# Low weight parts at another place within 64 bytes than the moving rows, in a hybrid encoder layer on one core

## The chip, the cores and the metric

The kernel runs on one core of a Trainium2 chip. The metric is the device time of one execution in microseconds, as the median of several runs.

## The reference

One layer: a gated Hyena branch (long convolution by FFT) and an attention branch on one normalised input, merged by sigmoid gates, projected, and followed by a SwiGLU FFN. All arrays are float32: 512 tokens, width 2048, FFN width 5632.

```python
h = rms_norm(x, mix_norm_g)
u_h, q, k, v, g = split(h @ w_in)
y_h = hyena(u_h)                        # short conv, product, long FFT conv, product
y_a = block_gqa_attention(rope(norm(q)), rope(norm(k)), v)
g_h, g_a = split(sigmoid(g + b_gate), 2)
x = x + (g_h * (y_h @ w_br_hyena) + g_a * (y_a @ w_br_attn)) @ w_out
h2 = rms_norm(x, ffn_norm_g)
return x + (silu(h2 @ w_ffn_gate) * (h2 @ w_ffn_up)) @ w_ffn_down
```

## The kernel before

All large products are made on TensorE in float32r, an operand being split into a high part and a low part (the rest). ScalarE copies the high part, VectorE subtracts it to get the low one, and TensorE multiplies high by high, high by low and low by high (`mm`, line 125). Weights come as tiles of 128x1024 numbers, eight blocks of 128x128, by DMAs on SyncE's queue (`raw` tiles).

Four stages use a scheme with seven products in place of eight, two by two blocks at a time (`seven`): the gates (names begin with g), the FFN's gate and up matrices (f), and the two halves of the FFN's down matrix (d and e). `run` goes through groups; a group takes four weight tiles (a11, a21, a22, a12), makes four sums of them on VectorE (`wsum`, line 868, tiles s), splits seven tiles (`wsplit`: ScalarE's copy on line 875, VectorE's subtraction on line 877), and runs seven products in three banks of PSUM called x, y and z. There are 15 groups in the gates, 44 in the FFN and 8 in each down half, so 75 groups and 525 products.

A product (`product`) has eight high matmuls, whose moving rows are 512 columns (256 of the high part of X and 256 of its low part, side by side), and eight low matmuls, whose weights are the low parts and whose moving rows are the 256 high columns. Each matmul has weights of its own, which are loaded ahead while the matmul before it streams. In the gates and in the FFN the order within a product turns from one product to the next (high, low; low, high; ...), but for the first and the last group; in the down halves it is always high, low. The instructions run in program order on each engine, and every split has a tile from a ring of three (`whi` and `wlo`, shared with the other stages, where `wblk` fills them).

Pools are filled from the left side of SBUF upwards and, later in the kernel, from the right side downwards. Each tile's place follows from what was allocated before it. Counting through the allocations, the tiles `wh`, `wl` and X all begin 32 bytes past a multiple of 64 bytes in every partition, and rows and blocks within them are multiples of 64 bytes long. (The word place means this remainder from here on.) One group of matmuls is otherwise: in the filters' transform (names kp), the constant tables CS, which are the weights there, lie at place 0, since a tile `fl` of 1296 bytes comes before them, and the moving rows kus and kvs lie at place 32. A small tile, `pad_t`, holds room on the right side.

Of the kernel before, what the change touches and what calls it, by code (L numbers as in the profile page):

```python
# [11 lines left out]
F32 = mybir.dt.float32  # L12
F32R = mybir.dt.float32r
# [4 lines left out]
P = 128  # L18
# [11 lines left out]
BLK = 8  # L30
# [16 lines left out]
O_ORDER = (4, 5, 6, 7, 8, 0, 9, 10, 11, 12, 1, 2, 3, 13, 14, 15)  # L47
STD_ORDER = (*range(EARLY_ACTS, NSTD), *range(EARLY_ACTS))
NEARLY = 5

C_X0, C_X1, C_HV, C_Q, C_KV, C_GH, C_GA = 0, 1024, 2048, 3072, 4096, 4608, 6656

# [54 lines left out]
def layer_kernel(tc, wpk, xT, par, flt, zemb, w4, decT, tbl, tb2, rope, qkg, out):  # L107
# [5 lines left out]
    wpool = tc.alloc_tile_pool(name="wpool", bufs=1)  # L113
# [46 lines left out]

    state = {"tile": 0, "pos": BLK, "hi": None, "lo": None}

    def wblk(nb=1):
        st = state
        if st["pos"] >= BLK:
            i = st["tile"]
            raw = wpool.tile([P, BLK * P], F32, tag="raw", bufs=2, name=f"wr{i}")
            hi = wpool.tile([P, BLK * P], F32R, tag="whi", bufs=3, name=f"wh{i}")
            lo = wpool.tile([P, BLK * P], F32R, tag="wlo", bufs=3, name=f"wl{i}")
            st.update(tile=i + 1, pos=0, hi=hi, lo=lo, raw=raw)  # L170

        i, n = st["tile"] - 1, {1: XW // 2, 2: XW}.get(st["tile"], BLK)
        if st["pos"] % n == 0:
            c = slice(st["pos"] * P, (st["pos"] + n) * P)
            nc.sync.dma_start(st["raw"][:, c], wpk[i, :, c])
            nc.scalar.copy(st["hi"][:, c], st["raw"][:, c])  # L176
            nc.vector.tensor_tensor(st["lo"][:, c], st["raw"][:, c], st["hi"][:, c].bitcast(F32), ALU.subtract)  # L177
        a = st["pos"] * P
        st["pos"] += nb
        return st["hi"][:, a:a + nb * P], st["lo"][:, a:a + nb * P]  # L180
# [6 lines left out]
    def group(ps, act, k0=0, k1=None):  # L187
        n = len(act)
        for k in range(k0, n if k1 is None else k1):
            wh, wl = wblk()  # L190
            mm3(ps, wh, wl, act[k][0], act[k][1], k == 0, k == n - 1)
            step()
# [312 lines left out]
    queue(mlp_gen())  # L505
    queue(filter_gen(0))
    w00 = wblk()
    for k in range(KT):
        xr = r3.tile([P, S], F32, tag="r", bufs=16, name=f"xr{k}")
        nc.sync.dma_start(xr, xT[k])  # L510
        hl = r1.tile([P, 2 * S], F32R, tag="hl", bufs=16, name=f"xh{k}")
        hi, lo = hl[:, :S], hl[:, S:]
        nc.scalar.activation(hi, xr, AF.Copy, scale=pcol("mixg", k))
        nc.vector.scalar_tensor_tensor(lo, xr, pcol("mixg", k), hi.bitcast(F32), ALU.mult, ALU.subtract)
        xg.append((hi, lo))
        for i in range(XW):
            wh, wl = wblk() if k + i else w00
            if k == 0:
                mm(xps[i], wh, hi, True, False)
                mm(xps[i], wl, hi, False, False)  # L520
                mm(xps[i], wh, lo, False, False)
            else:
                mm3(xps[i], wh, wl, hi, lo, False, k == KT - 1)
            step()
        sumsq_add(acc1, xr, k, "xsq", work)
# [88 lines left out]
    at = tc.alloc_tile_pool(name="at", bufs=1)  # L614
# [179 lines left out]
    def behind(ins):  # L794
        return tc.issue_after(ins) if ins else nullcontext()

    def seven(nm, gi, nv=3, turns=False):
# [25 lines left out]
        def x_tile(p):  # L823
            pool = xa if p < NEARLY else late["xb"][p - NEARLY]
            return pool.tile([P, 2 * SQ], F32R, tag="X", bufs=NEARLY if p < NEARLY else 1, name=f"{nm}X{p}")

# [13 lines left out]
        def x_split(p, V, cuts):  # L840
            xs[p] = x_tile(p)
            for a, b in zip(cuts, cuts[1:]):
                x_high(p, V, a, b)
                x_low(p, V, a, b)
# [20 lines left out]
        def wsum(name, a, b, ins=None):  # L865
            t = late["sg"].tile([P, BLK * P], F32, tag="sg", bufs=3, name=nm + name)
            with behind(ins):
                raws["sum"] = nc.vector.tensor_tensor(t, a, b, ALU.add).ins  # L868
            return t

        def wsplit(w, name, ins=None, low_ins=None):
            hi = wpool.tile([P, BLK * P], F32R, tag="whi", bufs=3, name=f"{nm}wh{name}")
            lo = wpool.tile([P, BLK * P], F32R, tag="wlo", bufs=3, name=f"{nm}wl{name}")
            with behind(ins):
                nc.scalar.copy(hi, w)  # L875
            with behind(low_ins):
                raws["wl"] = nc.vector.tensor_tensor(lo, w, hi.bitcast(F32), ALU.subtract).ins  # L877
            return hi, lo
# [31 lines left out]
        def run(groups, c_tiles, finish, rows=None, sums=None, side_pool=None, norm=None, tail=None, each=None, halves=False,  # L910
# [8 lines left out]
            def pool(name, **kw):  # L919
                return tc.alloc_tile_pool(name=nm + name, bufs=1, reuse_waits="tile", **kw)  # L920
# [7 lines left out]
            for n in range(groups):  # L928
# [4 lines left out]
                if tail and n == groups - 1:  # L933
                    next(tail)
                h11 = wsplit(w0["a11"], f"a11_{n}")
                if first:
                    for p in rows:
# [3 lines left out]

                    late["xb"] = [pool(f"xb{p}") for p in range(NP - 1, NEARLY - 1, -1)][::-1]
                    ready = NP - 1 if sums else NP
                    s1 = wsum(f"s1_{n}", w0["a21"], w0["a22"])
                    for p in range(NEARLY, ready):
                        x_split(p, V[p], (0, 7) if p < NP - 1 else (0, 3, 7))
                        if p == (NEARLY if sums else NP - 1):
                            s2 = wsum(f"s2_{n}", s1, w0["a11"], raws["xl"])
# [10 lines left out]
                if not first:  # L959
                    s1 = wsum(f"s1_{n}", w0["a21"], w0["a22"])  # L960
                hs1 = wsplit(s1, f"s1_{n}", raws["x"] if first else None)
                product(y, hs1, 2, True, 0, ready, swap=turn(n))
                if ready < NP:
                    V[ready] = sums()
                    v6 = raws["v6"]
                    x_split(ready, V[ready], (0, 3))
                    s4 = wsum(f"s4_{n}", s2, w0["a12"], v6)
                    x3 = raws["x"]
                    x_high(ready, V[ready], 3, 7)
                    product(x, h11, 0, True, ready)  # L970
                    product(y, hs1, 2, True, ready)
                    v1 = fold(f"v1_{n}", x)
                    x_low(ready, V[ready], 3, 4, raws["folda"])
                    hs2 = wsplit(s2, f"s2_{n}", x3, raws["xl"])
                    x_low(ready, V[ready], 4, 7, raws["wl"])
# [72 lines left out]
    yas = [split_row(r1, t, "hl", 16, f"yas{i}") for i, t in enumerate(ya)]  # L1048
    r3.release()
    pad = tc.alloc_tile_pool(name="pad", bufs=1, side="right", reuse_waits="tile")  # L1050
    pad_t = pad.tile([P, 112], F32, name="pad_t")
    nc.vector.memset(pad_t, 0.0)
    wq = tc.alloc_tile_pool(name="wq", bufs=1, side="right", reuse_waits="tile")
    xa = tc.alloc_tile_pool(name="xa", bufs=1, side="right", reuse_waits="tile")
# [4 lines left out]
    def x_rows(k):  # L1059
        t = tmp(f"xg{k}")  # L1060
        nc.scalar.dma_start(t, xT[k])
        nc.vector.tensor_tensor(t, t, rbc, ALU.mult)
        return t
# [3 lines left out]
    for m in range(KT):  # L1067
# [18 lines left out]
        if p is not None:  # L1086
            V[p] = x_sums(p, x_rows(2 * p), x_rows(2 * p + 1))
            if p < NEARLY:
                x_split(p, V[p], (0, 7))
# [68 lines left out]
    for k in range(KT):  # L1158
# [3 lines left out]
        for op in ops:  # L1162
            wh, wl = wblk()
# [246 lines left out]
```

## Time and profile before

| | |
|---|---|
| median of 3 runs | 2538.96 us (2538.38 to 2540.01) |
| the profiled execution's own time | 2538.14 us |
| its span, first to last instruction | 2536.3 us |
| granted TensorE clock | 1.00 |
| TensorE busy | 2524.7 us, 100% of the span, 13454 matmuls |
| weight loads busy | 2175.4 us, 86% |
| VectorE busy | 2049.9 us, 81% |
| ScalarE busy | 1198.8 us, 47% |
| GpSimd busy | 176.7 us, 7% |
| seven-product stages, begin to end | gates from some 750 to 1039 us, FFN 1225 to 2087, down halves 2164 to 2309 and 2380 to 2535 |

A row of a group of instructions reads: line, engine, operation, output and inputs by the program's names (the moving rows first, then the weights), shape, count; then busy time and the mean duration of one in ns; then idle time before it. The duration that the profile shows of a matmul runs on into the next one, so durations are longer than the spacing of two starts.

### The profile page before, as it was taken

The numbers are of one execution on the slowest core, as the hardware profiler recorded it, in microseconds if no ns is written. First come the engines' busy times: TensorE is split into PE (matmuls) and PEld (weight loads), VectorE is DVE, ScalarE is ACT, GpSimd is POOL, SyncE is SP. The second block draws the span as 40 slices with busy tenths as digits, with TensorE's granted clock in tenths as the row PEclk, the third lists the DMA queues.
The fourth block names the chain that finished last, engine by engine and source line by source line (L and its number), as shares of the span: only waits on it lengthen the run. The fifth ranks groups of instructions, "written<-read, shape, count | busy, mean of one in ns | idle before, by whom it ended". The sixth has DMA issues, their size and how long they took to land.

```text
span 2536.3 us, 35131 instructions
## 1 busy us (share of the span) xinstructions
PE 2524.7 (100%) x13454; PEld 2175.4 (86%) x13454; DVE 2049.9 (81%) x2949; ACT 1198.8 (47%) x1797; POOL 176.7 (7%) x291
## 2 busy tenths in 40 slices
PE   9999999999999999999999999999999999999999
PEld 7888888888888888888888888888888888888888
DVE  7878763766559999754899989999999988987987
ACT  6544433655445545543544444444444445445443
POOL 1000001110000000000000000000000002001111
PEclk9999999999999999999999999999999999999999
DMA  7333333222543444654333333333333338647754
GB/s 245 108 98 103 108 110 109 76 79 98 190 162 137 161 155 140 205 166 142 112 111 126 113 129 120 122 125 117 127 123 116 126 133 231 172 125 181 186 156 116
DMA packets 112899, 346.25 MB, mean 137 GB/s; under 512 B 13851, under 2 KB 15131, under 8 KB 112508
## 3 DMA queue, kind: packets, MB, share of 16 engines
q1 hardware_dynamic: 70128, 248.02, 29.4%
q0 software_dynamic: 22192, 59.00, 8.9%
q10 hardware_dynamic: 20412, 37.01, 4.7%
q8 instruction: 105, 1.72, 0.3%
q14 instruction: 62, 0.51, 0.1%
HBM read 295.47 MB, written 52.17 MB: 137 GB/s over the span
## 4 chain that ended last, share of the span: by engine, by line
PE 95%; DVE 3%; ACT 1%; issue 1%; POOL 0%; DMA 0%; SPq 0%; ACTq 0%; DVEq 0%
PE fx L125 19%; PE fy L125 10%; PE px L125 8%; PE o L125 7%; PE b L125 6%; PE gx L125 6%; PE d L125 5%; PE fz L125 5%; PE dx L125 3%; PE ex L125 3%; PE q L125 3%; PE gy L125 3%; PE phv L125 2%; PE ey L125 2%; PE kv L125 2%; PE dy L125 2%
## 5 line engine op out<-in xcount | busy, mean ns | idle before, releaser
L177 DVE TENSOR_TENSOR wl<-wr,wh 128x1024 fp32r<-128x1024 f32 (+1 forms) x168 | 200.9, 1197 | 152.2 <-ACT wh L176 149.2
L176 ACT CAST wh<-wr 128x1024 fp32r<-128x1024 f32 (+1 forms) x168 | 173.5, 1033 | 270.8 <-PE o L125 64.2
L875 ACT CAST fwhs<-fs 128x1024 fp32r<-128x1024 f32 x176 | 184.8, 1050 | 90.7 <-PE fz L125 68.8
L877 DVE TENSOR_TENSOR fwls<-fs,fwhs 128x1024 fp32r<-128x1024 f32 x176 | 214.5, 1219 | 14.8 <-ACT fwhs L875 14.8
L875 ACT CAST fwha<-fa 128x1024 fp32r<-128x1024 f32 x132 | 139.1, 1054 | 151.6 <-PE fx L125 83.5
L125 PE MATMUL px<-xh,wh 128*128 128x512 f32 x576 | 179.9, 393 | 0.1
L125 PE MATMUL fx<-fX,fwhs 128*128 128x512 f32 x704 | 175.3, 391 | 0.6 <-DVE fv L907 0.6
L125 PE MATMUL fy<-fX,fwhs 128*128 128x512 f32 x704 | 175.4, 391 | 0.0
L125 PE MATMUL fx<-fX,fwha 128*128 128x512 f32 x704 | 172.0, 391 | 1.3 <-DVE c L1004 1.3
L877 DVE TENSOR_TENSOR fwla<-fa,fwha 128x1024 fp32r<-128x1024 f32 x132 | 161.2, 1221 | 10.5 <-ACT fwha L875 10.2
L125 PE MATMUL o<-ms,wh 128*128 128x512 f32 x512 | 157.6, 389 | 0.0
L125 PEld LDWEIGHTS fx<-fX,fwha 128*128 128x128 f32 x704 | 129.2, 188 | 26.8 <-issue 1.9
L125 PEld LDWEIGHTS fx<-fX,fwhs 128*128 128x128 f32 x704 | 129.2, 188 | 25.9 <-DVE fv L907 0.9
L125 PEld LDWEIGHTS fy<-fX,fwhs 128*128 128x128 f32 x704 | 129.3, 188 | 24.9
L125 PEld LDWEIGHTS px<-xh,wh 128*128 128x128 f32 x576 | 105.9, 188 | 23.9 <-issue 2.4
L125 PE MATMUL d<-act,wh 128*128 128x512 f32 x384 | 118.3, 389 | 0.0
L125 PEld LDWEIGHTS o<-ms,wh 128*128 128x128 f32 x512 | 96.0, 188 | 19.8
L125 PE MATMUL px<-xh,wl 128*128 128x512 f32 x288 | 112.5, 391 | 0.0
L868 DVE TENSOR_TENSOR fs<-fa,fa 128x1024 f32<-128x1024 f32 x88 | 107.2, 1219 | 2.5 <-PE o L125 1.0
L868 DVE TENSOR_TENSOR fs<-fs,fa 128x1024 f32<-128x1024 f32 x88 | 107.2, 1218 | 0.9 <-PE o L125 0.2
L125 PE MATMUL o<-ms,wl 128*128 128x512 f32 x256 | 99.6, 389 | 0.0
L125 PE MATMUL fx<-fX,fwls 128*128 128x256 f32 x704 | 98.7, 283 | 0.2 <-DVE fwls L877 0.2
(1103 smaller groups left out, 5998.3 us busy)
## 6 DMA issues: line engine op xcount, KB each, us to landing
fa<-wpk SPq DMA_DIRECT2D x176, 512.0 KB, 3.6
wr<-wpk SPq DMA_DIRECT2D x162, 512.0 KB, 3.5
ga<-wpk SPq DMA_DIRECT2D x60, 512.0 KB, 4.3
da<-wpk SPq DMA_DIRECT2D x32, 512.0 KB, 4.3
ea<-wpk SPq DMA_DIRECT2D x32, 512.0 KB, 4.3
actd<-c POOLq DMA_DIRECT2D x41, 256.0 KB, 4.5
actr<-actd ACTq DMA_DIRECT2D x41, 256.0 KB, 4.5
x2d<-dt POOLq DMA_DIRECT2D x32, 256.0 KB, 5.4
```

What stands on the lines that cost most here:

```text
L125: tc.keep_in_program_order(nc.tensor.matmul(out, lhsT=lhsT, rhs=rhs, start=start, stop=stop, **kw))
L176: nc.scalar.copy(st["hi"][:, c], st["raw"][:, c])
L177: nc.vector.tensor_tensor(st["lo"][:, c], st["raw"][:, c], st["hi"][:, c].bitcast(F32), ALU.subtract)
L868: raws["sum"] = nc.vector.tensor_tensor(t, a, b, ALU.add).ins
L875: nc.scalar.copy(hi, w)
L877: raws["wl"] = nc.vector.tensor_tensor(lo, w, hi.bitcast(F32), ALU.subtract).ins
```

## The change

The low tiles of the four stages get 16 more numbers in a row (64 bytes), and the 1024 that are used begin at an offset of some floats. The offset is 8 in the gates and in the down halves. In the FFN it goes by the group's number modulo six: 8, 4, 12, 2, 6, 14. In groups 4 to 7 of the second down half the high parts begin at an offset of 4 floats as well. The places of the low parts thus become 0 (offset 8), 48 (4), 16 (12), 40 (2), 56 (6) and 24 (14). High tiles grow too, but stay at their place elsewhere. The pad becomes shorter by as much as the six tiles grow, 384 bytes.

```diff
+LOW_AT = {"g": (8,), "f": (8, 4, 12, 2, 6, 14), "d": (8,), "e": (8,)}
+HIGH_AT = 4
...
+    def w_tile(tag, name, at=0):
+        return wpool.tile([P, BLK * P + 16], F32R, tag=tag, bufs=3, name=name)[:, at:at + BLK * P]
+
     def wblk(nb=1):
...
-            hi = wpool.tile([P, BLK * P], F32R, tag="whi", bufs=3, name=f"wh{i}")
-            lo = wpool.tile([P, BLK * P], F32R, tag="wlo", bufs=3, name=f"wl{i}")
+            hi = w_tile("whi", f"wh{i}")
+            lo = w_tile("wlo", f"wl{i}")
...
         def wsplit(w, name, ins=None, low_ins=None):
-            hi = wpool.tile([P, BLK * P], F32R, tag="whi", bufs=3, name=f"{nm}wh{name}")
-            lo = wpool.tile([P, BLK * P], F32R, tag="wlo", bufs=3, name=f"{nm}wl{name}")
+            n = int(name.split("_")[1])
+            hi = w_tile("whi", f"{nm}wh{name}", HIGH_AT if nm == "e" and n >= 4 else 0)
+            lo = w_tile("wlo", f"{nm}wl{name}", LOW_AT[nm][n % len(LOW_AT[nm])])
...
-    pad_t = pad.tile([P, 112], F32, name="pad_t")
+    pad_t = pad.tile([P, 16], F32, name="pad_t")
```

## The prediction

> **What bounds the kernel now.** I read the page first: busy shares, the forty slices, the chain that ended last.
>
> ```profile
> span 2536.3 us, 35131 instructions
> PE 2524.7 (100%) x13454; PEld 2175.4 (86%) x13454; DVE 2049.9 (81%) x2949; ACT 1198.8 (47%) x1797; POOL 176.7 (7%) x291
> ...
> PEclk9999999999999999999999999999999999999999
> ...
> PE 95%; DVE 3%; ACT 1%; issue 1%; POOL 0%; DMA 0%; SPq 0%; ACTq 0%; DVEq 0%
> PE fx L125 19%; PE fy L125 10%; PE px L125 8%; PE o L125 7%; PE b L125 6%; PE gx L125 6%; PE d L125 5%; PE fz L125 5%; PE dx L125 3%; PE ex L125 3%; PE q L125 3%; PE gy L125 3%; PE phv L125 2%; PE ey L125 2%; PE kv L125 2%; PE dy L125 2%
> ```
>
> TensorE is never idle for long, its clock is granted in full in every slice, and the chain is TensorE for 95%. So the time is a number of matmuls times their spacing, and the change can act only through that spacing, unless it makes a helper late. Next, the stages that the change touches, as stretches (columns: the stretch, its us, then busy us and instructions of PE, PEld, DVE, ACT, POOL; granted clock, DMA share, GB/s):
>
> ```profile
> 780.00:1040.00 260.00, 259.59 (x1489) 228.35 (x1488) 241.20 (x323) 131.69 (x178) 7.57 (x14) 1.00 0.44 153
> 1600.00:2060.00 460.00, 460.00 (x2647) 406.61 (x2646) 418.75 (x544) 212.16 (x286) 12.98 (x24) 1.00 0.37 124
> 2170.00:2300.00 130.00, 130.00 (x745) 114.30 (x744) 117.98 (x157) 57.90 (x78) 12.12 (x14) 1.00 0.49 128
> ```
>
> Gates, FFN and down stage are all at TensorE's limit, with VectorE second at 91 to 93%. Then the groups of matmuls, kept apart by form (after the bar: busy us, mean ns of one):
>
> ```profile
> L125 PE MATMUL fx<-fX,fwha 128*128 128x512 f32 x704 | 172.0, 391 | 1.3 <-DVE c L1004 1.3
> L125 PE MATMUL o<-ms,wl 128*128 128x512 f32 x256 | 99.6, 389 | 0.0
> L125 PE MATMUL fx<-fX,fwls 128*128 128x256 f32 x704 | 98.7, 283 | 0.2 <-DVE fwls L877 0.2
> L125 PE MATMUL fy<-fX,fwls 128*128 128x256 f32 x704 | 98.6, 283 | 0.0
> L125 PE MATMUL fx<-fX,fwla 128*128 128x256 f32 x704 | 95.5, 283 | 0.0
> L125 PE MATMUL fz<-fX,fwla 128*128 128x256 f32 x352 | 49.2, 283 | 0.0
> L125 PE MATMUL kp<-kus01h,CS 128*128 128x512 f32 x4 | 1.6, 395 | 0.0
> L125 PE MATMUL ab<-T,Yt10h 128*128 128x256 f32 x8 | 1.6, 289 | 0.0
> ```
>
> A shown duration holds a tail that the next matmul overlaps. The size of the tail comes from the chain in order of time and from the timeline:
>
> ```profile
> 1050.38 174.11 PE o L125 x768
> ```
> ```profile
> 2171.72 1.12 PE L125 MATMUL dx<-dX,dwla 128*128 128x256 f32 x8
> 2172.67 2.00 PE L125 MATMUL dx<-dX,dwha 128*128 128x512 f32 x8
> 2174.51 1.11 PE L125 MATMUL dx<-dX,dwla 128*128 128x256 f32 x8
> 2175.46 0.40 PE L125 MATMUL dy<-dX,dwhs 128*128 128x512 f32 x1
> ```
>
> The output projection spaces its 512-column matmuls by 174.11/768 = 0.2267 us against 389 ns shown. Eight low matmuls of a down product take 0.95 us, 119 ns each, against some 282 shown. So spacing is duration less 163 ns, and a nanosecond in the mean duration of a group is a nanosecond of spacing. The eight high ones take 1.84 us, 230 ns each and not 227: each change from low to high rows costs 8 x 3 = 27 ns.
>
> **What the change removes, adds and moves.** No instruction, wait or DMA is added or taken away. Six weight tiles grow by 64 bytes; the pools behind them move by six times 64 and the pad gives the same 384 bytes back on the other side, so every other tile keeps its place within 64 bytes and its neighbours. The pad's memset, one instruction on VectorE, gets shorter and nobody waits for it.
>
> What moves is the place of the low weights: from 32 bytes past a 64-byte boundary, where the moving rows X lie too, to 0 (gates, down, and FFN groups n mod 6 = 0), and to 48, 16, 40, 56 or 24 in the other FFN groups. In the last four groups of the down stage's second half the high parts also go to 48.
>
> *Whom it touches.* A group has seven products of eight low matmuls. Gates have 15 groups, the FFN 44, the two down halves 8 each: 75 x 56 = 4200 low matmuls (the four f rows above sum to 2464 = 44 x 56). During nearly all of them the next low weights are loaded, now from another place than the rows that stream. About 333 changes from high to low (112 in the down halves, one per product; half as many as products where the order turns, 161 and 60) load low weights during a high matmul. The moved high parts are 4 x 56 = 224 matmuls.
>
> *Price: what the trace has of it.* One group of before has weights and moving rows 32 bytes apart: in kp, of the filters, the weights CS lie at place 0 and the rows kus and kvs at 32, by the order of allocation. All other float32r groups of this form have both at one place. The tile's own view (min/median/max ns):
>
> ```profile
> L125 PE MATMUL kp<-kus00h,CS x4: 392/394/397, 108.9 to 114.9; 128*128 128x512 f32 x4
> L125 PE MATMUL kp<-kus01h,CS x4: 395/395/395, 109.6 to 115.6; 128*128 128x512 f32 x4
> ```
> ```profile
> 108.93 0.39 PE L125 MATMUL kp<-kus00h,CS 128*128 128x512 f32 x1
> ...
> 110.32 0.62 PE L125 MATMUL px<-xh,wh 128*128 128x512 f32 x2
> ```
>
> Six kp matmuls take 1.39 us, 232 ns each, against 227: 395 against 389 shown, 6 ns more. They are 512 columns wide and come in runs of six, too short to show whether they would settle. So another place is not free in this trace, but the rows are not low matmuls. For those, the nearest rows are low products that have fallen out of their regular step, and the extremes of one group:
>
> ```profile
> L125 PE MATMUL gz<-gX,gwla 128*128 128x256 f32 x8 | 1.1, 283 | 0.0
> L125 PE MATMUL gx<-gX,gwls 128*128 128x256 f32 x8 | 1.1, 281 | 0.0
> ```
> ```profile
> L125 PE MATMUL fx<-fX,fwla x704: 277/283/363, 1225.9 to 2087.4; 128*128 128x256 f32 x176
> ```
>
> The first two rows are neighbouring products (us 965.5 to 967.5): in step 283, out of step 281. The 277 is the first low matmul after high ones, 6 ns below the step. Bounds per low matmul: below -6 (277), above +6 (kp against o, and 289 of ab<-T,Yt10h against 283). I take -1 ns. The 512-column rows at another place look like 512-column rows out of step: 392 to 397 for kp, and the eight high ones behind low ones average 163 + 230 = 393. So I carry over "out of step" and not "+6"; the out-of-step low row is -2, and I halve it because with six places some groups should fall into step again at 283.
>
> *Sum*, against the profiled execution's own 2538.14 us (span 2536.3 plus 1.8 around it; the median 2538.96 is 0.8 above):
> - low matmuls: 4200 x -1 ns = -4.2 us; bounds -25 and +25.
> - high matmuls that load moved low weights: 333 x 6 ns (kp) = +2.0 us; bounds 0 and +2.
> - moved high parts: 224 x 6 ns = +1.3 us, bounds 0 and +1.3.
> - the 27 ns of each change from low to high, 333 x 27 = 9 us in all: it is out-of-step time as well, so I leave it; bounds -9 (low rows leave TensorE in the high rows' step) and 0.
> - the first low matmul's 6 ns: 333 x 6 = 2 us, left; bounds 0 and +2.
> Together -0.9 us: 2537.2 for the profiled run, **2538 us** in the median, with ends at 2505 and 2570 if every term went one way.
>
> *Cover.* The low parts are written by VectorE at the new place:
>
> ```profile
> L877 DVE TENSOR_TENSOR fwls<-fs,fwhs 128x1024 fp32r<-128x1024 f32 x156 | 190.2, 1219 | 13.6 <-ACT fwhs L875 13.5
> ```
>
> No row shows such a write at another place. I cost it at nothing since VectorE is free for 460 - 418.75 = 41 us in the FFN stretch, which holds 460/19.5 = 23.6 groups and 165 such writes: each may grow by 0.25 us, a fifth, before VectorE sets the pace. Beyond that the sums and folds queued behind it come late, and TensorE waits for its weights; +0.1 us more per write would be 525 x 0.1 = 52 us. I see no row that asks for it.
>
> **The rule weighed.** Rows first: 395 ns (kp) against 389 (o) for the same shape, differing in place alone as far as I can tell. The Trainium skill, page "TensorE: Matmul & The Clock Gate", section "Step-by-step: what each phase is for", says that TensorE has two independent read ports and that loading the next weights takes no read bandwidth from the running matmul. By that rule the place could not matter and the sum would be 0: 2539. The trace disagrees by those 6 ns, so I give the rule's result a small chance of its own below.
>
> **Rivals.**
> *Slower: the kp price holds for low rows.* Each low matmul pays 6 ns as kp does: 25.2 + 2.0 + 1.3 + 2 = +30.5, 2569; if only some of the places pay, 2550 or so. For it: kp is the only place-to-place comparison, and a low matmul has its whole length covered by a load. Against it: kp looks like any unsettled run. It decides from 1.2 ns per low matmul on (5.1 us / 4200).
> *Faster: low rows keep the 277.* If another place lets load and rows pass each other, 4200 - 333 low matmuls gain 6 ns: -23, less the 3.3 that high ones pay: 2519; half the places, 2529. For it: 277 occurs in each run of low matmuls, so 6 ns are there to gain. Against it: it occurs only behind a high matmul, whose length had hidden the load.
> *Nothing: the place does not matter for low rows,* 2539, as the rule above has it. Against: kp.
> *Slower at places 40, 56 and 24 alone*, the ones that are no multiple of 16 bytes: no row shows a load from such a place. Loads differ little in before:
>
> ```profile
> L125 PEld LDWEIGHTS fx<-fX,fwha 128*128 128x128 f32 x704 | 129.2, 188 | 26.8 <-issue 1.9
> L125 PEld LDWEIGHTS fx<-fX,fwls 128*128 128x128 f32 x704 | 93.4, 191 | 4.3 <-DVE fwls L877 0.6 <-DVE fv L907 0.2
> ```
>
> If an odd place costs each load as much as these two differ, 3 ns on 21 FFN groups, 1176 low matmuls, is +3.5 on my sum: 2541.5. The Trainium skill, page "SBUF — State Buffer", section "Specifications (TRN2)", states 16-byte lines and a penalty for each cross to a new line; no run here shows it yet.
>
> **How the numbers follow.** My forecast (out of step, or in step again, by place; own range 2532 to 2544) 0.35; slower by the kp price, at all or some places, 0.30; faster by 277, at all or some places, 0.20; nothing 0.10; 8-byte places 0.05. This kernel's runs spread by 1.6 us, so I take 0.2%, 5.1 us, as what a measurement can tell from no change. The forecast's own range falls mostly inside it, a fifth below and a tenth above. Faster: 0.20 + 0.07 = 0.27. Slower: 0.30 + 0.03 + 0.02 = 0.35. Same: 0.38. The range goes to 2519, the faster rival in full, and to 2566, just short of the slower one in full; some 2 in 10 stay outside.
>
> **What would show it.** In the profile after, the f rows of low matmuls: 281 to 283 for the forecast, 289 for the slower rival, 277 for the faster. By stretches of one group (19.5 us) the six places stand apart. The row of high matmuls, 391 now: 389 if the changes from low to high settle sooner, 392 if the moved loads cost. The write of the low parts must stay near 1219 ns and VectorE under 95% of the FFN stretch. The prediction is wrong if low matmuls at one place settle at a spacing that no row of before shows, such as 127 or 113 ns throughout.

## The result, and the profile after

The changed kernel takes 2559.36 us in the median of 4 runs (2558.53 to 2560.54), against 2539.49 us for the kernel before on the same chips. The ratio is 1.0079, with a 95% interval from 1.0061 to 1.0096. It is slower by 20 us, where 2538 had been forecast. The profiled execution's own time is 2560.54 us.

The page of the changed kernel, lines as shown of before:

```profile
span 2558.7 us, 35131 instructions
PE 2545.7 (99%) x13454; PEld 2170.8 (85%) x13454; DVE 2053.0 (80%) x2949; ACT 1197.4 (47%) x1797; POOL 175.6 (7%) x291
...
PEclk9999999999999999999999999999999999999999
...
PE 95%; DVE 2%; ACT 1%; issue 1%; DMA 0%; SPq 0%; ACTq 0%; DVEq 0%
```

The clock, the instruction count and the chain are as before: TensorE for 95%. Nearly all of the 22 us of span are spacing of matmuls; 1.4 are one wait at 1878 us, which the profile puts down to VectorE's fv (the row of fy below). The groups by form say which (two rows of before that were not shown yet, then the same and more of after):

```profile
L125 PE MATMUL px<-xh,wh 128*128 128x512 f32 x576 | 179.9, 393 | 0.1
L125 PE MATMUL d<-act,wh 128*128 128x512 f32 x384 | 118.3, 389 | 0.0
```
```profile
L127 PE MATMUL px<-xh,wh 128*128 128x512 f32 x576 | 182.1, 397 | 0.2 <-ACT xh L518 0.2
L127 PE MATMUL d<-act,wh 128*128 128x512 f32 x384 | 120.2, 394 | 0.0
L127 PE MATMUL o<-ms,wl 128*128 128x512 f32 x256 | 101.0, 395 | 0.0
L127 PE MATMUL fx<-fX,fwha 128*128 128x512 f32 x704 | 173.8, 393 | 1.3 <-DVE c L1010 1.3
L127 PE MATMUL fx<-fX,fwls 128*128 128x256 f32 x704 | 97.6, 281 | 0.2 <-DVE fwls L883 0.2
L127 PE MATMUL fy<-fX,fwls 128*128 128x256 f32 x704 | 97.6, 280 | 1.4 <-DVE fv L913 1.4
L127 PE MATMUL fx<-fX,fwla 128*128 128x256 f32 x704 | 94.1, 280 | 0.0
```

The reader sees two things. The low rows of the FFN (fwls, fwla), which the change moves, became shorter: 283 to 280 and 281. And rows that the change does not speak of became longer by 4 to 6 ns: px, d and o. In the chain of waits o is one piece, and the ordinary part of the down matrix, d, is two (before, then after):

```profile
2087.65 65.31 PE d L125 x288
2309.71 65.31 PE d L125 x288
```
```profile
1060.57 178.16 PE o L127 x768
2106.40 66.81 PE d L127 x288
2330.00 66.83 PE d L127 x288
```

o went from 174.11 to 178.16 us, d from 130.62 to 133.64. Adding up the trace's spacing from start to start by stage gives the whole account of the two profiled executions, in us (the second row holds the 5 us from the last matmul's start to the end of the span as well):

| stages | before | after | difference |
|---|---|---|---|
| seven products: FFN f | 861.4 | 865.9 | +4.5 |
| seven products: gates, two down halves | 614.0 | 614.9 | +1.0 |
| plain products (px, b, o, d, q, phv, kv, gates' ahead) | 900.1 | 917.2 | +17.1 |
| all else | 159.4 | 159.3 | -0.2 |

So three quarters of the loss is where no low part was moved within its tile. All 3936 matmuls of the plain products have 512 moving columns, so each pays 17.1/3936 = 4.3 ns.

What these stages share with the change is the growth of the six weight tiles. The allocations give how far each weight tile begins from the moving rows, modulo 256 bytes (the distance, from here on). Before: 0 for all six. After: 128, 192 and 0 for the three high tiles, and 64, 128 and 192 for the three low ones, since each tile shifts the next by 64 bytes and all six shift the rows by 384. Modulo 64 all of these are 0, which is why the prediction saw no move.

### The profile page after: what moved, and what is told of

It is laid out like the page before. It is cut to its first block, busy times and chain, and to the rows that moved or that the text cites. A ratio compares the mean times of both kernels' runs of the same rounds, so it can differ in the third digit from the quotient of the medians.

```text
span 2558.7 us, 35131 instructions
## 1 busy us (share of the span) xinstructions
PE 2545.7 (99%) x13454; PEld 2170.8 (85%) x13454; DVE 2053.0 (80%) x2949; ACT 1197.4 (47%) x1797; POOL 175.6 (7%) x291
## 4 chain that ended last, share of the span: by engine, by line
PE 95%; DVE 2%; ACT 1%; issue 1%; DMA 0%; SPq 0%; ACTq 0%; DVEq 0%
PE fx L127 19%; PE fy L127 10%; PE px L127 8%; PE o L127 7%; PE b L127 6%; PE gx L127 6%; PE d L127 5%; PE fz L127 5%; PE dx L127 3%; PE ex L127 3%; PE q L127 3%; PE gy L127 3%; PE phv L127 2%; PE ey L127 2%; PE kv L127 2%; PE dy L127 2%
## 5 line engine op out<-in xcount | busy, mean ns | idle before, releaser
L127 PE MATMUL fy<-fX,fwls 128*128 128x256 f32 x704 | 97.6, 280 | 1.4 <-DVE fv L913 1.4
```

Source lines behind the costliest of these rows:

```text
L127: tc.keep_in_program_order(nc.tensor.matmul(out, lhsT=lhsT, rhs=rhs, start=start, stop=stop, **kw))
```

## The experiments

In the expectations, A is the theory that the unit of distance is 128 bytes, D that it is 256 (or 512) bytes, B that the low parts' places within 64 bytes are what costs, C that any growth or shift costs, E that only unequal tiles in a ring cost, and F that the order of places in a survey, not the place, makes its numbers. Differences by stage below are sums of spacing against before, as in the table.

**grow64_only.** The tiles grow as in the change; every offset is 0.

```diff
-LOW_AT = {"g": (8,), "f": (8, 4, 12, 2, 6, 14), "d": (8,), "e": (8,)}
-HIGH_AT = 4
+LOW_AT = {"g": (0,), "f": (0,), "d": (0,), "e": (0,)}
+HIGH_AT = 0
```

> The tiles grow by 64 bytes as in the change, but all low and high parts stay at offset 0, so nothing is moved within 64 bytes. Theory A (what counts is the place within 128 bytes: by the growth, every second weight tile lies 64 bytes off the moving rows, in all stages): the output projection and the other stages keep the 394 to 397 ns of the change's profile, total 2554 to 2560 us. Theory B (what counts is the place within 64 bytes, so the loss comes from the moved low parts): 389 and 283 ns throughout, total 2539 us. Theory C (any tile stride other than 4096 bytes, or any shift of the pools, costs): as A.

Measured: 2559.34 us (2558.03 to 2561.99), ratio 1.0076 (1.0063 to 1.0089). Groups by form:

```profile
L127 PE MATMUL d<-act,wh 128*128 128x512 f32 x384 | 120.1, 394 | 0.0
L127 PE MATMUL o<-ms,wl 128*128 128x512 f32 x256 | 101.0, 394 | 0.0
L127 PE MATMUL fx<-fX,fwha 128*128 128x512 f32 x704 | 174.2, 394 | 1.3 <-DVE c L1010 1.3
L127 PE MATMUL fx<-fX,fwls 128*128 128x256 f32 x704 | 97.6, 281 | 0.2
```

These are the rows of after to 1 ns. Plain products +16.6, sevens +7.6 us. The growth alone makes the whole loss; B fell.

**grow128_only, grow128_places, survey_low.** The high tiles stay as before and the low ones grow by 128 bytes, so the rows shift by 384 again: high tiles lie 128 off, low tiles 128, 0, 128. Offsets 0; the change's low offsets; and a survey of offsets.

```diff
+        more = 32 if tag == "wlo" else 0
+        return wpool.tile([P, BLK * P + more], F32R, tag=tag, bufs=3, name=name)[:, at:at + BLK * P]
...
+LOW_AT = {"g": (0,), "f": (0,), "d": (0,), "e": (0,)}                              # grow128_only
+LOW_AT = {"g": (8,), "f": (8, 4, 12, 2, 6, 14), "d": (8,), "e": (8,)}              # grow128_places
+LOW_AT = {"g": (0,), "f": tuple(range(0, 34, 2)), "d": (16,), "e": (16,)}          # survey_low
```

> High tiles as before, low tiles longer by 128 bytes (three of them, so the pools behind move by the same 384 bytes as in the change), all parts at offset 0. The low tiles are now 4224 bytes apart, and the weights lie 128 bytes or 256 off the moving rows. Theory A: every matmul back at 389 (512 columns) and 283 (256 columns, in step), total 2539 us within 2. Theory B: the same. Theory C: the output projection at 394 or more, total 2550 or more.

> As the kernel with low tiles longer by 128 bytes, but the low parts of the seven-product stages at the change's offsets (8 floats in gates and down, 8, 4, 12, 2, 6, 14 by FFN group; high parts unmoved). Theory A: projection and other stages at 389, the seven-product stages within some 6 us of before, so 2539 to 2546 us. Theory B: the whole loss is there, 2555 to 2560 us. Theory C: 2550 or more, with the projection at 394.

> Low tiles longer by 128 bytes; the FFN's groups take offsets 0, 2, 4, ... 32 floats in turn (17 places, 2 to 3 groups each), gates 0, down halves 16 floats (64 bytes). Theory A: offsets 0 and 32 give 19.27 and 19.35 us a group (the two orders) as in before, 16 is as far off as the others, 281 to 283 for low and 391 to 396 for high matmuls; the down halves at 64 bytes off lose their regular step. Theory B: 0, 16 and 32 alike, the down halves unchanged at 282. Theory C: all groups alike, slower than before.

Measured: 2572.84 us, ratio 1.0131 (1.0117 to 1.0145); 2569.29 us, ratio 1.0115 (1.0099 to 1.013); and one run of 2567.36 us. Of grow128_only, chain and groups:

```profile
1064.29 178.82 PE o L127 x768
```
```profile
L127 PE MATMUL o<-ms,wl 128*128 128x512 f32 x256 | 101.3, 396 | 0.0
L127 PE MATMUL fx<-fX,fwha 128*128 128x512 f32 x704 | 175.1, 395 | 1.2 <-DVE c L1011 1.0
L127 PE MATMUL fx<-fX,fwls 128*128 128x256 f32 x704 | 98.6, 283 | 0.2 <-DVE fwls L884 0.2
```

128 bytes are not a place like 0: they are worse than the change's mixture. A fell. Plain products were +19.7 us in all three kernels; the sevens were +15.1, +11.3 and +9.6. With the high weights off, other low places give back a part, no more.

**rows256, rows512.** The tiles are as before; a gap behind the weight rings moves everything that comes after them by 256 or 512 bytes. (For 512 the table `ngain` is cut to the columns that are used, to make room. It lies ahead of the weights, so weights and rows both begin 128 bytes further modulo 256 than before. The same is so in low32, places256, the two surveys with high weights in step, and low88 and low76_o.)

```diff
+            if i == 0:
+                gap(64, "gap_c")    # floats; 128 in rows512
```

> The kernel before with a gap of 256 bytes behind the weight rings (the pad gives them back on the right): weights all stay where they were, every moving row lies 256 bytes further on, in all stages. Theory D256 (weights and moving rows keep the regular step when their places agree within 256 bytes): 389 and 283 ns, 2539 to 2541 us. Theory D512 (they must agree within 512 bytes, the length of a row of a 128x128 weight block): no group is in step, projection 394 to 396 as in the kernel whose low tiles are 128 bytes longer, total 2560 to 2575 us. Theory E (only unequal places of the tiles of one ring cost, not their distance from the rows): 2539 to 2541 us.

> The same with a gap of 512 bytes (384 of them from a constant tile whose unused columns are cut). Theories D256 and D512: in step, 389 and 283 ns, 2539 to 2541 us. Theory C (any shift of the pools costs): 2555 or more.

Measured: 2540.63 us, ratio 1.0002 (0.9992 to 1.0011), and 2539.04 us, ratio 0.9996 (0.9987 to 1.0005). Of rows256:

```profile
1051.08 174.11 PE o L125 x768
```
```profile
L125 PE MATMUL o<-ms,wl 128*128 128x512 f32 x256 | 99.6, 389 | 0.0
```

o is what it was before, to 0.01 us. A shift by itself costs nothing, so C fell, and 256 bytes are as good as 0: the unit is 256 at most, while 128 was not 0. D with 256 stands.

**low32.** As rows512, but 32 of the 512 bytes lie ahead of the low tiles. So all low parts, in every stage, lie 32 bytes off, the high ones 0, and the tiles of each ring are equal.

```diff
+            if i == 0:
+                gap(8, "gap_b")     # ahead of the low ring
...
+                gap(120, "gap_c")   # behind it
```

> The kernel before with gaps of 32 bytes ahead of the ring of low weights and 480 behind it, so that low weights lie 32 bytes off the moving rows in all stages and everything else keeps its place within 512 bytes. The change's idea by itself. Theory D: the low matmuls of the seven-product stages at 281 to 283, their high ones at 390 to 392, so these stages within 5 us of before; in the other stages, where each third load is a low one, the regular step is lost and 512-column matmuls go to 391 to 395: total 2548 to 2560 us. Theory E: all tiles of a ring agree, so 2539 to 2541 us.

Measured: 2559.88 us, ratio 1.0078 (1.0065 to 1.0091). Plain products +20.4 us, sevens +1.4. Chain and groups:

```profile
1061.90 179.20 PE o L125 x768
```
```profile
L125 PE MATMUL o<-ms,wh 128*128 128x512 f32 x512 | 162.0, 398 | 0.0
L125 PE MATMUL o<-ms,wl 128*128 128x512 f32 x256 | 99.6, 389 | 0.0
L125 PE MATMUL fx<-fX,fwha 128*128 128x512 f32 x704 | 173.2, 392 | 1.3 <-DVE c L1014 1.3
L125 PE MATMUL fx<-fX,fwls 128*128 128x256 f32 x704 | 97.8, 281 | 0.2 <-DVE fwls L887 0.2
```

E fell: the rings are even. In o the trace repeats a cycle of three starts, 233, 239 and 228 ns apart, where before had 226.7 throughout. Each third load comes from 32 bytes off, and all three matmuls pay 6.6 ns in the mean. The duration shown puts the whole on the high rows (398 against 389) and nothing on the low ones (389), so a single row would mislead; the chain's 179.20 us does not.

This run also has the prediction's own case in it. The sevens, with low parts 32 off and high parts at 0, have low rows of 281 and high rows of 392.

**places256.** The change's low places alone: low tiles grow by 256 bytes, so each of the six tiles is again a multiple of 256 bytes from the rows; high parts are not moved.

```diff
+            lo = wpool.tile([P, BLK * P + 64], F32R, tag="wlo", bufs=3, name=f"{nm}wl{name}")[:, at:at + BLK * P]
...
+LOW_AT = {"g": (8,), "f": (8, 4, 12, 2, 6, 14), "d": (8,), "e": (8,)}
```

> The change's low places alone (8 floats in gates and down, 8, 4, 12, 2, 6, 14 by FFN group), the high parts not moved, and every tile a multiple of 256 bytes from the moving rows, so that all other stages keep their spacing. The forecast's sum for the seven-product stages without the moved highs was -0.9 - 1.3 = -2.2 us: 2537 to 2539. Theory D, with the survey's products at 8, 24 and 32 bytes (2764, 2794, 2797 ns against 2784 at 0) and the places 16, 40, 48 and 56 taken as between them: within 10 ns x 525 = 5 us of before, 2536 to 2545, with all other stages unchanged to 0.5 us each. Rival B (the low parts' places are what makes the changed kernel slow): 2555 to 2560.

Measured: 2538.44 us (11 runs), ratio 0.9993 (0.9985 to 1.0002). Plain products -0.2 us, sevens +0.9, in which the down halves' waits are longer by some 2.3. Groups:

```profile
L126 PE MATMUL o<-ms,wl 128*128 128x512 f32 x256 | 99.6, 389 | 0.0
L126 PE MATMUL fx<-fX,fwha 128*128 128x512 f32 x704 | 172.6, 392 | 1.4 <-DVE c L1006 1.4
L126 PE MATMUL fx<-fX,fwls 128*128 128x256 f32 x704 | 97.7, 281 | 0.2 <-DVE fwls L879 0.2
```

The places that the change is about make no measurable difference in the whole, within the 2537 to 2539 of the forecast's sum. By place they do differ: a product of the FFN took 2785 ns in before and here, for places 0, 16, 24, 40, 48 and 56, 2786, 2777, 2771, 2764, 2790 and 2790 ns (means without the products that hold a wait). That nearly cancels over the six. The low tiles also lie 4352 bytes apart here and not 4096, so a tile length other than 4096 bytes costs nothing by itself, which was the other half of C. The 20 us come with the distances that the growth made.

**survey_low_step, survey_fine.** High weights in step; the FFN's low parts at a new place in each group.

```diff
+LOW_AT = {"g": (0,), "f": tuple(range(0, 34, 2)), "d": (8,), "e": (24,)}           # low tiles + 128 bytes: 0, 128, 0 off
+LOW_AT = {"g": (0,), "f": (17, 18, 19, 20, 21, 22, 23, 24, 25, 38, 46, 54, 56, 60), "d": (22,), "e": (22,)}   # + 256: all 0
```

> High weights in step (gaps as in the kernel with 512 bytes); low tiles 4224 bytes apart, so that the three lie 0, 128 and 256 bytes off the rows, and FFN groups add 0, 8, 16, ... 128 bytes in turn (gates none, down halves 32 and 96). By group and tile the low matmuls show every eighth byte from 0 to 384. Theory D: low matmuls at 0 in step (283), all others 279 to 289, on average 281 to 282; high matmuls between low ones 390 to 394. D256: 256 is as good as 0; D512: it is not. Theory E: no group in step in any stage.

> A survey: all weight tiles in step with the moving rows modulo 256 bytes, low parts of the FFN groups in turn at 68, 72, 76, 80, 84, 88, 92, 96, 100, 152, 184, 216, 224 and 240 bytes past them; gates, down 88 or 0. Theory D expects the product's time to depend on the place smoothly or by 8-byte steps with its least near 88 (2746 ns), 80 and 96 between 2760 and 2780; rival F (order in the survey, not the place) expects all within 2765 to 2795 with no minimum at 88. Total 2530 to 2540.

Measured: one run each, 2540.63 and 2534.36 us. In the first, o shows the unit once more: its chain row is

```profile
1053.48 175.17 PE o L126 x768
```

and the spacing was 226.7 ns in the tiles at 0 and at 256 bytes, 231.1 in those at 128. Time of one product by distance of its low parts, in ns, each the mean of several products of the FFN (those over 2840 ns, which hold a wait, are left out):

| distance, bytes | high first | low first | from |
|---|---|---|---|
| 0 | 2766 | 2798 | survey_low_step |
| 24 | 2791 | 2796 | survey_low_step |
| 32 | 2770 | 2803 | survey_low_step |
| 64 | 2759 | 2767 | survey_low_step |
| 88 | 2742 | 2751 | survey_low_step |
| 128 | 2782 | 2777 | survey_low_step |
| 76 | 2742 | 2747 | survey_fine |
| 84 | 2787 | 2813 | survey_fine |
| 152 | 2750 | 2774 | survey_fine |

(The expectations' 2797 at 32 bytes mixed in products of the down halves, which always take the high part first and are slower; in the FFN alone 32 lies at 2787 in the mean of the two orders.) The expected smooth curve with its least near 88 did not come: 84 lies between the two best places and is worse than 0. By what rule the distance counts is not known from these runs.

**low88, low76_o.** The best places of the surveys for all seven-product stages. In low76_o the low parts of o were moved too, to see whether 512 moving columns have good places of their own.

```diff
+LOW_AT = {"g": (22,), "f": (22,), "d": (22,), "e": (22,)}                          # low88
+LOW_AT = {"g": (19,), "f": (19,), "d": (19,), "e": (19,)}                          # low76_o
+O_AT = {i: 19 if i < 184 else 22 for i in range(168, 200)}                         # low76_o, tiles of o
```

> All weight tiles lie a multiple of 256 bytes from the moving rows; only the low parts of the seven-product stages lie 88 bytes further. Theory D (the distance between the weights that are loaded and the rows that stream, modulo 256 bytes, sets the spacing) takes its price from the survey of low places: at 88 bytes a product took 2742 (high first) and 2751 ns (low first), at 0 bytes 2770 and 2798, so 38 ns less on 75 x 7 = 525 products: -20 us, 2520 (2514 to 2527), the low rows' spacing at 114 to 116 instead of 119 ns, and the 512-column stages o, px, b, q, kv unchanged at 227. Rival B (the place within 64 bytes, here 24) expects what the changed kernel's groups at 24 had: 19.30 us a group instead of 19.31, so 2539 to 2540. Rival F (the survey's products at 88 were short only because they stood between products at other places, two of each) expects 2536 to 2541.

> Low parts of the seven-product stages 76 bytes past the moving rows modulo 256, and in the output projection o (512 moving columns, 32 weight tiles) the low parts of the first sixteen tiles 76 bytes past, of the last sixteen 88 bytes past; all else in step. Theory D by the fine survey: a product at 76 bytes 2735 (high first) or 2747 ns (low first) against 2770 and 2801 at 0, 44 ns x 525 = -23 us for the sevens; they settle in one cycle as at 88 bytes, since the neighbours now lie alike. For o two ways are open: wide rows have good places too, then the spacing falls below 226.7 ns in the trace (to 222 or so, o -3 us, total 2513 to 2516); or any place but 0 breaks a step of 226.7 that is already the wide rows' best, then o costs what it cost at 32 bytes, 233.3 ns or +5 us (total 2521), or less by a part. Rival F (order of places in the survey) expects sevens at 76 no better than at 0: 2540 to 2545.

Measured: low88 2522.76 us (2521.24 to 2524.38), ratio 0.9936 (0.9923 to 0.995); low76_o 2524.28 us, ratio 0.9942 (0.9929 to 0.9956). Both beat the kernel before. Of low88, span, chain, groups and a stretch of the timeline:

```profile
span 2519.4 us, 35131 instructions
```
```profile
1048.07 174.10 PE o L126 x768
```
```profile
L126 PE MATMUL fx<-fX,fwha 128*128 128x512 f32 x704 | 171.9, 391 | 1.4 <-DVE c L1006 1.4
L126 PE MATMUL fx<-fX,fwls 128*128 128x256 f32 x704 | 95.4, 278 | 0.2
L126 PE MATMUL fy<-fX,fwls 128*128 128x256 f32 x704 | 95.3, 277 | 0.0
```
```profile
1701.88 1.09 PE L126 MATMUL fx<-fX,fwls 128*128 128x256 f32 x8
1702.80 1.07 PE L126 MATMUL fz<-fX,fwla 128*128 128x256 f32 x8
1703.71 2.00 PE L126 MATMUL fz<-fX,fwha 128*128 128x512 f32 x8
```

Eight low matmuls take 0.92 and 0.91 us by their starts, against 0.95 before, and the high rows stay at 391. Sevens -17.4 us, plain products -0.1. F fell. The gain is short of the 20 expected: the FFN gained 11.9 us, as its 308 products at 38 ns would, but the gates and the down halves 5.6 instead of 8.2. All products of the down halves take the high part first, and there one gains some 26 ns (from 2793 to 2767) and not 38. Behind high matmuls the first four low ones are not yet in the new step (intervals 121, 116, 119, 118, then 113 and 114). Of low76_o:

```profile
1047.69 177.93 PE o L127 x768
```
```profile
L127 PE MATMUL o<-ms,wh 128*128 128x512 f32 x512 | 159.9, 393 | 0.0
L127 PE MATMUL fx<-fX,fwls 128*128 128x256 f32 x704 | 95.1, 277 | 0.2
```

Its sevens gain 18.8 us (23 expected), and o loses 3.8: 231.1 ns at 76 bytes, 232.2 at 88. The places that are best for the low matmuls of the sevens cost in o. These runs do not tell whether that is its 512 columns or its mixture, since in o only each third load is a low one and in the sevens eight low ones follow each other. With o left at 0 and 76 bytes for the sevens, the sum would be about 1 us below low88; that kernel was not run.

## Why the prediction was wrong

**The step that failed.** It is the sentence "Six weight tiles grow by 64 bytes; the pools behind them move by six times 64 and the pad gives the same 384 bytes back on the other side, so every other tile keeps its place within 64 bytes and its neighbours", and the nothing at which it costed the growth. The places within 64 bytes do stay; the unit that counts is 256 bytes (rows256, grow128_only, survey_low_step). The growth put five of six weight tiles off by 64, 128 or 192 bytes, in every stage. grow64_only has the loss without any moved low part, and places256 has the moved low parts without the loss.

**The price was at hand.** The prediction read 395 against 389 from kp and o and took 6 ns for a 512-column matmul with weights at another place. For o that was nearly right: after's o shows 394 and 395, its spacing in the mean 178.16/768 = 232.0 against 226.7, 5.3 ns. The prediction laid it on 333 + 224 matmuls. On the 3936 of the plain products it would have been 23.6 us, and 2562. That this lies near 2559 is in part luck: the plain products paid 4.3 ns in the mean and not 6, and the sum leaves out the loss of the sevens. What failed was the count of the matmuls that pay, since 64 bytes had been taken for the unit without a row to show it: kp's 32 bytes do not tell 64 from 256.

**The other terms.**
- Low matmuls: -1 ns each was taken; the FFN's spacing (waits left out, here and below) went from 119.5 to 118.0 in after, to 118.3 in places256, 118.2 in low32. The shown 280 and 281 lie at or just below the forecast's 281 to 283.
- High matmuls: in places256, where only low weights are moved, the FFN's high matmuls went from 228.5 to 229.1 ns (2464 x 0.6 = 1.5 us) and the gates' from 229.0 to 230.5 (840 x 1.5 = 1.3 us); with the down halves that is 3.2 us in all, against 2.0 forecast for all 75 groups, which was also given as the upper bound. The row of high matmuls shows 392 there, the sign that the prediction named for moved loads that cost. In after the FFN's went to 231.1, +2.7 ns x 2464 = 6.6 us, and grow64_only, with no low part moved, has 231.5: that loss came with the growth, which put high and low weights off by 64, 128 and 192. That, and the one wait of 1.4 us, is why the sevens together lost 5.5 us and did not gain 0.9.
- Moved high parts: the 1.3 us were not measured apart; in after they lie among matmuls whose weights the growth had put off.
- Cover: VectorE's write of the low parts did not change with the place. The group's row in after:

```profile
L883 DVE TENSOR_TENSOR fwls<-fs,fwhs 128x1024 fp32r<-128x1024 f32 x176 | 214.6, 1219 | 14.6 <-ACT fwhs L881 14.6
```

**The rivals.** "Slower: the kp price holds for low rows" had the side and about the size, by another mechanism: low rows gained and wide rows paid. "Faster: low rows keep the 277" was false for the change's places and true for another: low88 shows 277 and 278 in the low rows of the FFN, and 2522.8 us against the 2519 that this rival gave. "Slower at places 40, 56 and 24 alone" did not come: by its 3 ns on each of eight low matmuls these three places would take 24 ns more a product than the other three, and in places256 they take 9 less, 2775 against 2784. "Nothing", the rule of two independent read ports (the Trainium skill, page "TensorE: Matmul & The Clock Gate", section "Step-by-step: what each phase is for"), would have all kernels here at 2539. The runs lie between 2523 and 2573 with the same matmuls, so what the prediction drew from the rule, that the place cannot matter, does not hold for the spacing of these float32r matmuls with a new weight load each. Whether a load takes read bandwidth from the matmul, or is held up itself, the traces do not show.

**What stays open.** That it is the distance of weights and moving rows, and not the weights' own address, follows from low88: there the rows lie 128 bytes further modulo 256 than in before and so do the weights of the plain products, and these keep their time. Nor is it that weights must lie alike among themselves: in grow128_only every third weight tile of o follows one that lies as it does itself, with all high and low weights 128 bytes from the rows, and its 24 matmuls are 232.6 ns apart in the mean against 226.7. What within the chip has 256 bytes was not seen; the traces show starts and ends alone.

## What to carry to other kernels

In a kernel like this one, with TensorE busy all the time and a weight load for each float32r matmul, growing or shifting a tile that lies ahead of the weights or the moving rows can be an edit to every stage: count the distance modulo 256 bytes, not 64, and keep it where it is by padding to 256. Price an edit on all matmuls whose distance it alters, not only on those that it names. A survey that gives each group another place costs one run and found 17 us that the intended places did not have.

## What the runs showed of the hardware

Where all matmuls settle at one spacing, the trace's starts give 226.7 ns for 512 columns in before, 120.0 for 256 columns, and 113.3, just half of 226.7, for 256 columns at 76 or 88 bytes. All three are multiples of 6.67 ns (34, 18 and 17). Elsewhere the spacing goes round in a cycle: of three starts in low32's o, with a mean of 233.3, and of seven in grow128_only's o where all weights lie 128 bytes off, with a mean of 232.4. Intervals in ns:

```
o, before:  227 226 227 227 226 227 227 226 227 227 226 227
o, low32:   233 239 228 233 239 228 233 239 228 233 239 228
f, before:  (high) 227 226 | (low) 114 119 120 120 120 120 120 120
f, low88:   (high) 227 226 | (low) 121 116 119 118 113 114 113 113
```

So a settled low matmul in before was 6.7 ns longer than one at 88 bytes. The gain of low88 comes from there: the FFN's low matmuls went from 119.5 to 114.7 ns in the mean, 2464 x 4.8 = 11.8 of its 11.9 us.
